# DeltaNet's inversion fed from keys and gates alone, its decays built early, and ones on TensorE in the first norm

## The chip, the cores and the metric

The kernel runs on one core of one Trainium2 chip. The metric is the device time in microseconds of one execution, the median over several. A profiled execution comes with a trace: every instruction of the engines PE (TensorE), ACT (ScalarE), DVE (VectorE) and POOL (GpSimd) and of the DMA queue SP (SyncE), with its start, duration and what ended the idle time before it.

## What is computed

A model of two layers on 512 tokens of width 1024 (batch 1): in the first a gated DeltaNet beside a dilated attention, in the second a retention beside a long convolution, and behind each a convolutional feed-forward network. The DeltaNet is what the change is about. Cut to one direction (g is the sum of the log gates within a chunk, beta the write gate):

```python
q, k, v = silu(dwconv(h @ w_in))          # q and k are normalised per head
a   = strict_lower((k * beta) @ k.T * exp(g_i - g_j))
u,w = solve(a + I, [v * beta, k * beta * exp(g)])
intra = lower(q @ k.T * exp(g_i - g_j))
for each chunk:
    v_new = u - w @ state
    o     = (q * exp(g)) @ state + intra @ v_new
    state = state * exp(g_last) + (k * exp(g_last - g)).T @ v_new
y = rmsnorm(o) * silu(z)
```

Both directions run, and their outputs are added. The result is multiplied by `ab_w_out` and added to x.

## The kernel before

**Products.** Matmuls are made exact enough by splitting each operand into a rounded part (hi) and a rest (lo); one product is three matmuls (`mm3`, L262). The activations come transposed (`hh`, `hl`). A weight tile of 128x1024 is loaded to `raw` (SP), cast to `whi` by ACT (`fetch`, L253) and `wlo` is the difference, made by DVE or, where `pool_lo` is set, by POOL (L254). There are four buffers each of `whi` and `wlo` and three of `raw`; a projection of 128 columns (`ap` or `gup`) is 24 matmuls.

**Start.** `K.start` (L190) is the one part whose instructions run in the order in which they are written. The norm's weight row is spread over 128 partitions by two matmuls with a row of ones (`nrowp`, L91), six transposes of the identity follow (`warm`, L188), each token tile is squared (ACT, L128), its factor made (POOL, L129 and L130), scaled (DVE, `xn`, L139), transposed (PE, `nt`, L152) and split (`hh` by ACT, `hl` by DVE), and the first projections (`first`) begin.

**DeltaNet.** Everywhere else a scheduler of the framework sets the order on each engine, from the order in which the code is written and the data each step needs. Twelve tiles are projected: four of keys, four of queries, four of values. Each goes through a convolution (`conv3`: ACT L362, then DVE L365 and L366), Silu (ACT), and a transpose (PE, `tp`, L685); for keys and queries the norm is squared on ACT (L692, four instructions with a sum each), its root made on POOL (L386, L387), and applied on DVE (L697). Between the value tiles stand, per chunk c, the transposes of keys and queries (L765), the products `kkp` and `kqp` (L771, L773), the decays `dps` (PE) and their Exp (ACT, L783), and `blocks` (L785): the intra-chunk matrix A (DVE, L787), P = kk·beta·decay (DVE, L791, eight small instructions per chunk) and its 32x32 blocks to `Bt` (ACT L797, DVE L799). After the last chunk comes the recursion that inverts all 32x32 blocks at once (L824 and L825, 31 steps of two instructions on DVE, each needing the one before), its two transposes Y (L829, L830), then on PE the joining of blocks to 64 and 128 (`m32`, `m32b`, `m64`, `m64b`) and the recurrence over four steps. The gate projection `pt` (96 matmuls of `proj_tok`) stands ahead of the recursion in the code. The other half of the mixer's output product (`oacc`, eight units of 12 matmuls, `fill`) is spread over the places that `FILLS` counts: three units before `m32`, two before `m32b`, and so on.

The gates themselves (`gates`, L580) end in `G4` (L646), the log gates with both signs; `gate_operands` (L651) turns that into the operands of the decays, `gst` (eight ACT instructions, L672) in a buffer of `raw`.

## Time and profile before

| | us |
|---|---|
| median of 3 runs | 1341.88 (1340.59 to 1343.12) |
| the profiled execution | 1342.41 |
| its span, first to last instruction | 1340.6 |
| PE busy | 1311.6 (98%) |
| DVE busy | 752.0 (56%) |
| ACT busy | 531.7 (40%) |
| POOL busy | 152.8 (11%) |
| mean granted TensorE clock | 0.992 |

Busy times are of the whole span. PE has little idle time, so what the profile can show of a gain is in its waits, in its clock and in work that is taken away. The start covers 0 to 24 us of the span, the DeltaNet 139 to 345.

### The profile page before, as it was taken

What the parts mean: (1) busy time and instruction counts of PE and PEld (TensorE: products, weight loads), DVE (VectorE), ACT (ScalarE), POOL (GpSimd) and SP (SyncE); (2) the same over time, 40 slices, a digit from 0 to 9 for tenths busy, and PEclk for the clock granted to TensorE, in tenths of its full rate; (3) what the DMA queues carried; (4) which work ended last, traced back from release to release, by engine and by line L of the source; (5) the groups of instructions that cost most, each with busy time, mean ns of one, the idle gap of its engine ahead of it and who ended that gap; (6) DMA issues with size and microseconds to landing.
All of it is one profiled execution on the core that took longest, in us unless ns stands there. A gap on an engine that the chain in (4) does not pass through costs nothing.

```text
span 1340.6 us, 17716 instructions
## 1 busy us (share of the span) xinstructions
PE 1311.6 (98%) x6977; PEld 1098.2 (82%) x6977; DVE 752.0 (56%) x1106; ACT 531.7 (40%) x892; POOL 152.8 (11%) x182
## 2 busy tenths in 40 slices
PE   7999999899999999999999999999999999999997
PEld 6877887789888888888889787888898888888886
DVE  6677549968654432344436737769764443244432
ACT  4466567233443331233326424432443332133332
POOL 3454120003100000000001302024000000000002
PEclk9999999989999999999999999999999999999999
DMA  7431113221233333333333413321143333243321
GB/s 219 128 92 36 51 32 110 80 96 54 85 110 95 95 96 102 102 94 95 95 94 128 133 40 90 95 80 46 48 144 103 100 95 94 74 118 101 101 79 63
DMA packets 161027, 123.69 MB, mean 92 GB/s; under 512 B 6985, under 2 KB 134477, under 8 KB 160944
## 3 DMA queue, kind: packets, MB, share of 16 engines
q1 hardware_dynamic: 160798, 122.49, 31.2%
q8 instruction: 55, 0.90, 0.3%
q14 instruction: 28, 0.23, 0.1%
q10 hardware_dynamic: 146, 0.07, 0.0%
HBM read 117.30 MB, written 2.10 MB: 89 GB/s over the span
## 4 chain that ended last, share of the span: by engine, by line
PE 84%; DVE 8%; ACT 3%; issue 2%; DMA 1%; POOL 1%; SPq 1%; POOLq 0%; ACTq 0%; DVEq 0%
PE gup L265 11%; PE gup L266 11%; PE gup L267 11%; PE oacc L266 8%; PE oacc L265 8%; PE oacc L267 7%; PE hap L267 1%; PE ap L267 1%; PE hap L266 1%; PE ap L265 1%; PE ap L266 1%; PE hap L265 1%; PE first L266 1%; PE first L267 1%; PE first L265 1%
## 5 line engine op out<-in xcount | busy, mean ns | idle before, releaser
L254 DVE TENSOR_TENSOR wlo<-raw,whi 128x1024 fp32r<-128x1024 f32 x191 | 235.5, 1234 | 318.2 <-ACT whi L253 312.3
L253 ACT CAST whi<-raw 128x1024 fp32r<-128x1024 f32 (+1 forms) x197 | 206.5, 1049 | 432.8 <-PE gup L266 186.6
L267 PE MATMUL gup<-hh,wlo 128*128 128x512 f32 x656 | 255.6, 390 | 0.0
L266 PE MATMUL gup<-hl,whi 128*128 128x512 f32 x656 | 255.6, 390 | 0.0
L265 PE MATMUL gup<-hh,whi 128*128 128x512 f32 x656 | 255.6, 390 | 0.0
L267 PEld LDWEIGHTS gup<-hh,wlo 128*128 128x128 f32 x656 | 123.2, 188 | 25.7
L266 PEld LDWEIGHTS gup<-hl,whi 128*128 128x128 f32 x656 | 123.2, 188 | 25.3
L265 PEld LDWEIGHTS gup<-hh,whi 128*128 128x128 f32 x656 | 123.2, 188 | 25.3
L265 PE MATMUL oacc<-whi,ghi 128*128 128x512 f32 x352 | 137.3, 390 | 0.0
L267 PE MATMUL oacc<-whi,glo 128*128 128x512 f32 x352 | 137.2, 390 | 0.0
L266 PE MATMUL oacc<-wlo,ghi 128*128 128x512 f32 x352 | 137.1, 390 | 0.0
L267 PEld LDWEIGHTS oacc<-whi,glo 128*128 128x128 f32 x352 | 66.1, 188 | 13.8
L266 PEld LDWEIGHTS oacc<-wlo,ghi 128*128 128x128 f32 x352 | 66.1, 188 | 13.6
L265 PEld LDWEIGHTS oacc<-whi,ghi 128*128 128x128 f32 x352 | 66.1, 188 | 13.5
L429 DVE TENSOR_TENSOR sl<-gup,sl 128x512 f32<-128x512 f32 x42 | 29.1, 692 | 82.2 <-PE gup L267 82.2
L314 DVE TENSOR_TENSOR x<-oacc,x 128x512 f32<-128x512 f32 x64 | 43.5, 687 | 53.5 <-PE oacc L267 53.3
L428 ACT ACTIVATE sl<-c 128x512 f32<-128x512 f32 x44 | 27.8, 632 | 89.3 <-DVE c L366 89.3
L265 PE MATMUL first<-hh,whi 128*128 128x256 f32 x192 | 55.1, 289 | 0.0
L266 PE MATMUL first<-hl,whi 128*128 128x256 f32 x192 | 54.6, 285 | 0.2 <-DVE hl L226 0.2
L267 PE MATMUL first<-hh,wlo 128*128 128x256 f32 x192 | 54.5, 284 | 0.0
L265 PE MATMUL pt<-whi,hh 128*128 128x512 f32 x128 | 50.4, 394 | 3.7 <-ACT rt L454 2.5
L104 POOL TENSOR_SCALAR ss<-ss 128x1 f32<-128x1 f32 x16 | 5.0, 311 | 429.3 <-ACT jk L102 429.3
(403 smaller groups left out, 2361.9 us busy)
## 6 DMA issues: line engine op xcount, KB each, us to landing
raw<-in_ffn_w_in_dram SPq DMA_DIRECT2D x88, 512.0 KB, 3.9
raw<-in_ffn_w_out_dram SPq DMA_DIRECT2D x44, 512.0 KB, 3.7
raw<-in_ab_w_in_dram SPq DMA_DIRECT2D x28, 512.0 KB, 3.8
raw<-in_cd_w_in_dram SPq DMA_DIRECT2D x24, 512.0 KB, 4.0
x<-in_x_dram SPq DMA_DIRECT2D x16, 256.0 KB, 5.9
raw<-in_ab_w_out_dram SPq DMA_DIRECT2D x8, 512.0 KB, 3.7
raw<-in_cd_w_out_dram SPq DMA_DIRECT2D x8, 512.0 KB, 3.8
rs<-rt SPq DMA_DIRECT2D x48, 64.0 KB, 2.0
```

Source lines behind the costliest of these rows:

```text
L104: nc.gpsimd.tensor_scalar(ss[:, 1:2], ss[:, 0:1], s, EPS, op0=ALU.add, op1=ALU.add)
L253: self.nc.scalar.copy(hi, raw)
L254: (self.nc.gpsimd if self.pool_lo else self.nc.vector).tensor_tensor(lo, raw, hi, op=ALU.subtract)
L265: mm(out, a[0], b[0], start=start, stop=False)
L266: mm(out, a[0], b[1], start=False, stop=False)
L267: mm(out, a[1], b[0], start=False, stop=stop)
L314: self.nc.vector.tensor_add(xs, acc, xs)
L428: nc.scalar.activation(sl, c, AF.Silu)
L429: nc.vector.tensor_mul(sl, up, sl)
```

## The change

Four edits, of which the diff below shows the core.

- In the first norm the vector of ones is a 128x128 tile, and PE multiplies it by itself 6 times ahead of `nrowp`, 5 times behind it and 7 times behind the first transposes (`WARM`), in place of the six transposes of the identity. ACT loads the norm row before the identity and runs a 4-column Square (`tab`) before x arrives. The first weight's `wlo` is made by DVE in two halves between the scalings.
- Beta goes into the exponent of the decays (`gnl` = Ln of 1 + e), so P is one multiplication per direction and chunk, and the state's key factor takes beta (`eRb`); the multiplication of `vn` by beta becomes a copy on ACT. The mask of the diagonal goes.
- The sum of squares is one ACT instruction and a reduction on DVE.
- The DeltaNet's steps are written in another order: `gate_operands` and all decays behind the second key tile, with the decays put where A will stand; keys' products and P beside the query tiles; the recursion behind the value tiles and the gate projection in the code; A made in place beside the value tiles. `FILLS` puts no unit before `m32` and one at each later place.

```diff
         for h in range(2):
             p = k.wk(nm="nrowp")
...
+        k.warm_up(one, WARM[1])
...
+        n.scale(1, (0,))
+        lo = self.fetch(2)
+        n.turn(0, (0,))
+        self.warm_up(n.one, WARM[2])
+        lo.pop(0)()
+        n.turn(1, (0,))
+        n.scale(1, (1,))
+        n.turn(0, (1,))
+        lo.pop(0)()
+        n.turn(1, (1,))
...
+        nl = T("gnl")
+        nc.scalar.activation(nl, e, AF.Ln)
...
-            for cc in range(4):
-                jk = self.sm.tile([128, 128], F32, tag="jk2", name="jk2", bufs=1)
-                nc.scalar.activation(jk, tp[:, cc, :], AF.Square, accum_out=ss[:, cc:cc + 1])
+            nc.scalar.activation(jk, tp, AF.Square)
+            V.tensor_reduce(ss, jk, axis=AX.X, op=ALU.add)
...
-                    for h in range(4):
-                        V.scalar_tensor_tensor(P[d][:, 4 * c + h, :], kks[c][:, h, :], self.beta[:, c, 4 * d + h:4 * d + h + 1], dt[:, h, :], op0=ALU.mult, op1=ALU.mult)
+                    V.tensor_tensor(P[d][:, 4 * c:4 * c + 4, :], kkp, dt(c, d), op=ALU.mult)
...
+            tile(1, 0)
+            self.gate_operands(dp)
+            tile(1, 1)
+            turn()
             for c in range(4):
...
                 decays(c)
-                blocks(c)
+            for h in (2, 3):
+                tile(1, h)
+                turn()
+            tile(0, 0)
+            turn()
+            self.pool_lo = True
+            tile(0, 1)
+            turn()
+            for c in range(4):
+                heads_t(kT, Kt, c)
+            blocks(0)
+            tile(0, 2)
+            turn()
+            blocks(1)
+            blocks(2)
+            tile(0, 3)
+            turn()
+            blocks(3)
+            self.pool_lo = False
...
+            for h in range(4):
+                tile(2, h)
+                turn()
+                if h:
+                    attend(h)
+            turn()
+            attend(0)
+            self.proj_tok(n, lambda t, a: nc.scalar.activation(Zt[:, t, :], a, AF.Silu))
             for j in range(31):
...
-                    V.tensor_tensor(vn[d], vp, bc(self.beta[:, c, 4 * d:4 * d + 4, None], [128, 4, 128]), op=ALU.mult)
+                    nc.scalar.copy(vn[d], vp)
...
-FILLS = (3, 2, 0, 1, 1, 0, 0, 0, 1)
+FILLS = (0, 1, 1, 1, 1, 1, 1, 1, 1)
...
-WARM = 6
+WARM = (6, 5, 7)
```

`heads_t` is the old transpose of keys or queries and its copy on ACT (L768 of the changed kernel); `scores` the four products of a chunk (`kx`); `attend(c)` turns the queries, makes their products and multiplies them into the decays in place (L794 of the changed kernel).

The scheduler's order changes with the code. On PE, at the start, the rows before (`warm` on the identity, `nt` the transposes of the scaled tiles, `first` the first projection):

```order
L91 MATMUL nrowp<-nrow_97,one_99 128x512 x2
L188 MATMUL warm<-ident 128x128 x6
L152 MATMUL nt<-ident,xn 128x128 x16
L265 MATMUL first_201<-hh_133,whi 128x256
L266 MATMUL first_201<-hl_135,whi 128x256
```

and now:

```order
L192 MATMUL warm<-one_99 128x128 x6
L95 MATMUL nrowp<-nrow_96,one_99 128x512 x2
L192 MATMUL warm<-one_99 128x128 x5
L157 MATMUL nt<-ident,xn 128x128 x4
L192 MATMUL warm<-one_99 128x128 x7
L157 MATMUL nt<-ident,xn 128x128 x8
L278 MATMUL first_218<-hh_139,whi 128x256
```

Eighteen multiplications of ones stand where six transposes stood, seven of them between the first four transposes and the next eight, and the first projection begins after twelve transposes instead of sixteen.

On ACT, from the gates' Exp through the first key tiles (`eg` the gates, `scr` a tile under convolution or Silu, `jk` the squares, `whi` a weight's cast), before:

```order
L638 ACTIVATE eg<-gp 128x96
L649 ACTIVATE G_1580<-gp 128x32 x4
L362 ACTIVATE scr<-ap,dncw 128x512
L707 ACT_TABLE_LOAD
L707 ACTIVATE scr<-scr 128x512
L253 CAST whi<-raw 128x1024
L362 ACTIVATE scr<-ap,dncw 128x512
```

and the same place now, from the gates' operands on (`gx` and `gst` are these operands, `A` the tiles in which the decays are put):

```order
L231 CAST gx<-gt_1616 128x128
L689 COPY scr<-gx 32x128 x2
L728 ACT_TABLE_LOAD
L728 ACTIVATE scr<-scr 128x512
L689 COPY scr<-gx 32x128 x2
L694 ACTIVATE gst<-scr,gsel 128x128 x8
L375 ACTIVATE scr<-ap,dncw 128x512
L713 ACTIVATE jk<-tp 128x512
L260 CAST whi<-raw 128x1024
L762 ACT_TABLE_LOAD
L762 ACTIVATE A_1546<-dps 128x512
L728 ACT_TABLE_LOAD
```

The cast that stood one Silu behind the first convolution now stands behind the gates' operands, the second convolution and a Square; it is the weight of the third key tile, the next that PE projects.

On DVE, at the beginning of the recursion (`tm` and `scr` are its two instructions, L365 and L366 a convolution, `L` the transposed blocks), before:

```order
L365 SCALAR_TENSOR_TENSOR scr<-ap,dncw,scr 128x511
L812 STREAM_TRANSPOSE L<-Bt 128x1024
L366 SCALAR_TENSOR_TENSOR scr<-ap,dncw,scr 128x511
L254 TENSOR_TENSOR wlo<-raw,whi 128x1024
L824 TENSOR_TENSOR tm<-L,scr 128x31
L825 TENSOR_TENSOR scr<-scr,tm 128x31
```

and now in the middle of it (L378 and L379 are the convolution of the last value tile, L841 and L842 the recursion):

```order
L842 TENSOR_TENSOR scr<-scr,tm 128x16x16
L841 TENSOR_TENSOR tm<-L,scr 128x255
L267 TENSOR_TENSOR wlo<-raw,whi 128x1024
L378 SCALAR_TENSOR_TENSOR scr<-ap,dncw,scr 128x511
L842 TENSOR_TENSOR scr<-scr,tm 128x15x17
L379 SCALAR_TENSOR_TENSOR scr<-ap,dncw,scr 128x511
L794 TENSOR_TENSOR A_1549<-kx,A_1549 128x512
L794 TENSOR_TENSOR A_1546<-kx,A_1546 128x512
```

The last value tile's convolution, which ended before the recursion began, now stands behind 33 of its 62 instructions.

## Rows read from the trace of the kernel before

**Rows 1.** The waits of PE over the whole span, by what released it: us in total, times, longest.

```profile
PE m L855 <- DVE Y L829: 3.0, 1, 3.0
PE nt L152 <- DVE xn L139: 2.8, 1, 2.8
PE kkp L771 <- ACT kT L766: 2.1, 3, 1.4
PE pt L265 <- DVE scr L366: 1.2, 1, 1.2
```

**Rows 2.** The timeline of the start, all engines: start us, duration, engine, line, operation, and in brackets the idle time before and what ended it.

```profile
4.48 1.28 ACT L128 ACT_TABLE_LOAD   x1 [4.48 <-DMA x<-in_x_dram]
...
8.28 1.41 DVE L139 SCALAR_TENSOR_TENSOR xn<-x,ss,nrow 128x512 f32<-128x512 f32 x2
...
10.07 2.35 POOL L254 TENSOR_TENSOR wlo<-raw,whi 128x1024 fp32r<-128x1024 f32 x1
10.14 3.48 DVE L139 SCALAR_TENSOR_TENSOR xn<-x,ss,nrow 128x512 f32<-128x512 f32 x2 [0.46 <-POOL ss L130]
...
13.02 2.82 PE L152 MATMUL nt<-ident,xn 128*128 128x128 f32 x12 [2.83 <-DVE xn L139]
```

**Rows 3.** The timeline of PE at the first projection.

```profile
15.49 0.56 PE L265 MATMUL first<-hh,whi 128*128 128x256 f32 x1
...
16.49 0.28 PE L266 MATMUL first<-hl,whi 128*128 128x256 f32 x1
```

**Rows 4.** The timeline of ACT from the gates' Ln to the first key tiles, the last gate rows first.

```profile
136.72 0.58 ACT L526 COPY pT<-tp 128x512 f32<-128x512 f32 x1
...
145.72 1.28 ACT L638 ACT_TABLE_LOAD   x1
147.01 0.25 ACT L638 ACTIVATE eg<-gp 128x96 f32<-128x96 f32 x1
...
147.47 0.73 ACT L362 ACTIVATE scr<-ap,dncw 128x512 f32<-128x512 f32 x1
```

**Rows 5.** Groups of ACT from 139 to 268 us: line, engine, operation, shapes, count, busy us and mean ns of one, and idle time before.

```profile
L253 ACT CAST whi<-raw 128x1024 fp32r<-128x1024 f32 x16 | 16.8, 1052 | 19.7 <-PE ap L266 11.0 <-PE pt L267 8.6
...
L707 ACT ACTIVATE scr<-scr 128x512 f32<-128x512 f32 x9 | 5.7, 632 | 3.8 <-DVE scr L366 3.5
...
L672 ACT ACTIVATE gst<-scr,gsel 128x128 fp32r<-128x128 f32 x8 | 2.4, 388 | 0.0
```

**Rows 6.** Groups of DVE in the same stretch, same columns.

```profile
L254 DVE TENSOR_TENSOR wlo<-raw,whi 128x1024 fp32r<-128x1024 f32 x16 | 19.6, 1222 | 12.3 <-ACT whi L253 12.2
...
L791 DVE SCALAR_TENSOR_TENSOR P<-scr,beta 128x128 f32<-128x128 f32 x32 | 8.7, 346 | 0.0
L365 DVE SCALAR_TENSOR_TENSOR scr<-ap,dncw,scr 128x511 f32<-128x511 f32 x10 | 7.5, 747 | 6.2 <-ACT scr L362 6.1
...
L787 DVE TENSOR_TENSOR A<-kqp,scr 128x512 f32<-128x512 f32 x8 | 5.1, 685 | 1.6 <-ACT scr L783 1.6
L799 DVE STREAM_TRANSPOSE Bt<-P 32x128 f32<-32x128 f32 x16 | 4.8, 301 | 0.2
...
L812 DVE STREAM_TRANSPOSE L<-Bt 128x1024 f32<-128x1024 f32 x1 | 2.0, 2031 | 0.0
```

**Rows 7.** Windows of 20 us: busy us (x instructions) of PE, its weight loads, DVE, ACT, POOL, then granted clock (1.00 is 2.4 GHz, 0.50 is 1.2 GHz), DMA share, GB/s; and one window of 1 us behind the wait for the recursion.

```profile
180.00:200.00 20.00, 19.30 (x94) 15.75 (x93) 7.97 (x12) 11.94 (x45) 5.59 (x12) 1.00 0.05 14
200.00:220.00 20.00, 18.08 (x117) 15.60 (x117) 17.87 (x39) 15.40 (x30) 0.00 (x0) 1.00 0.29 82
220.00:240.00 20.00, 18.60 (x97) 15.36 (x96) 18.97 (x46) 14.68 (x25) 0.00 (x0) 1.00 0.41 130
240.00:260.00 20.00, 20.00 (x90) 16.58 (x89) 18.82 (x41) 5.44 (x7) 1.04 (x1) 1.00 0.30 84
...
277.00:278.00 1.00, 1.00 (x4) 0.81 (x3) 1.00 (x2) 0.00 (x0) 0.00 (x0) 0.50 0.16 57
```

**Rows 8.** The timeline of DVE through the recursion: its first instruction, the 34th of 62, and the transpose that PE waits for, which follows the last.

```profile
236.15 0.21 DVE L824 TENSOR_TENSOR tm<-L,scr 128x31 f32<-128x31 f32 x1
...
252.69 0.43 DVE L825 TENSOR_TENSOR scr<-scr,tm 128x255 f32<-128x255 f32 x1
...
264.47 1.90 DVE L829 STREAM_TRANSPOSE Y<-scr 128x1024 f32<-128x1024 f32 x1
```

**Rows 9.** The timeline of PE at the same place: fills before the wait, the joining of blocks, fills behind it.

```profile
261.66 0.39 PE L265 MATMUL oacc<-whi,yh 128*128 128x512 f32 x1
...
263.02 0.39 PE L265 MATMUL oacc<-whi,yh 128*128 128x512 f32 x1
266.43 2.00 PE L855 MATMUL m<-Y,P 32*32 32x32 f32 x64 [3.02 <-DVE Y L829]
...
276.47 0.63 PE L265 MATMUL oacc<-whi,yh 128*128 128x512 f32 x1
...
278.60 0.63 PE L267 MATMUL oacc<-whi,yl 128*128 128x512 f32 x1
```

**Rows 10.** The timeline of PE: the transposes behind two tiles that are five tiles apart.

```profile
163.50 0.60 PE L685 MATMUL tp<-ident,scr 128*128 128x128 f32 x4
...
193.09 0.60 PE L685 MATMUL tp<-ident,scr 128*128 128x128 f32 x4
```

**Rows 11.** The group of PE from 139 to 268 us for the keys' products of the four chunks (columns as in rows 5).

```profile
L771 PE MATMUL kkp<-kT 128*128 128x128 f32 x32 | 4.5, 285 | 2.1 <-ACT kT L766 2.1
```

More of the change, by code (lines that the diff above doesn't have):

```diff
@@ L85, in spread @@
         nc.scalar.dma_start(row, self.src)
-        one = k.sm.tile([1, 128], F32, tag="jk2", name="one1", bufs=1)
+        nc.scalar.dma_start(k.ident, k.I["ident"])
+        one = k.sm.tile([128, 128], F32, tag="jk2", name="one1", bufs=1)
         nc.vector.memset(one, 1.0)
+        nc.scalar.activation(k.sm.tile([128, 4], F32, tag="ss", name="tab", bufs=8), one[:, :4], AF.Square)
+        self.one = one
+        k.warm_up(one, WARM[0])
         self.w = k.cst.tile([128, D], F32, tag="nrow", name="nrow")
@@ L90, in spread @@
             p = k.wk(nm="nrowp")
-            nc.tensor.matmul(p, one, row[:, h * 512:h * 512 + 512], start=True, stop=True)
+            nc.tensor.matmul(p, one[:1], row[:, h * 512:h * 512 + 512], start=True, stop=True)
             nc.vector.tensor_copy(self.w[:, h * 512:h * 512 + 512], p)
+        k.warm_up(one, WARM[1])
     def square(self, t, c0=0):
@@ L136, in scale @@
         xn = self.xn[t]
-        for h in range(2):
+        for h in hs:
             sl = slice(h * 512, h * 512 + 512)
@@ L182, in new_x, with warm_up @@
         return self.cst.tile([128, NT, D], F32, tag="x", name=nm)
-    def warm_up(self, n):
+    def warm_up(self, one, n):
         p = self.wk((128, 128), "warm")
         for _ in range(n):
-            self.nc.tensor.transpose(p, self.ident, self.ident)
+            self.nc.tensor.matmul(p, one, one, start=True, stop=True)
     def start(self, n):
@@ L195, in start @@
         n.spread()
-        self.warm_up(WARM)
         n.whole(0)
@@ L253, in fetch @@
             self.nc.scalar.copy(hi, raw)
+            n = shape[1] // max(parts, 1)
+            cut = [slice(n * i, n * i + n) for i in range(parts)]
+            later = [lambda c=c: self.nc.vector.tensor_tensor(lo[:, c], raw[:, c], hi[:, c], op=ALU.subtract) for c in cut]
+            if parts:
+                self.ready.append((hi, lo))
+                return later
             (self.nc.gpsimd if self.pool_lo else self.nc.vector).tensor_tensor(lo, raw, hi, op=ALU.subtract)
@@ L754, in deltanet @@
             Ai = [dp.tile([128, 2, 4, 128], F32, tag="ai", name=f"A{st}", bufs=4) for st in range(4)]
-            prep = self.delta_prep(dp, n, gates, Kt, Qt, Vt, Zt)
-            next(prep)
-            self.gate_operands(dp)
+            tile, turn = self.delta_tiles(dp, n, gates, (Qt, Kt, Vt))
             Bt = self.xp.tile([128, 32, 32], F32, tag="xn", name="Bt")
-            kks, kqs, dts = {}, {}, {}
-            def turn(c):
-                for out, src in ((kT, Kt), (Qt, Qt)):
-                    tp = self.wk((128, 4, 128), "tp")
-                    for h in range(4):
-                        nc.tensor.transpose(tp[:, h, :], src[:, c, h, :], self.ident)
-                    nc.scalar.copy(out[:, c], tp)
-            def products(c):
-                kkp, kqp = self.wk((128, 4, 128), "kkp"), self.acc((128, 4, 128), "kqp")
-                for h in range(4):
-                    nc.tensor.matmul(kkp[:, h, :], kT[:, c, h, :], kT[:, c, h, :], start=True, stop=True)
-                for h in range(4):
-                    nc.tensor.matmul(kqp[:, h, :], kT[:, c, h, :], Qt[:, c, h, :], start=True, stop=True)
-                kks[c], kqs[c] = self.s2h("kk"), kqp
-                V.tensor_tensor(kks[c], kkp, bc(self.tri[:, 4:5, :], [128, 4, 128]), op=ALU.mult)
+            dt = lambda c, d: Ai[3 - c if d else c][:, d]
             def decays(c):
@@ L781, in decays, with heads_t, scores @@
                     nc.tensor.matmul(ps, self.gst[:, 4 * d + c, :], self.gmv, start=False, stop=True)
-                    dts[c, d] = self.s2h("dt")
-                    nc.scalar.activation(dts[c, d], ps, AF.Exp)
+                    nc.scalar.activation(dt(c, d), ps, AF.Exp)
+            def heads_t(out, src, c):
+                tp = self.wk((128, 4, 128), "tp")
+                for h in range(4):
+                    nc.tensor.transpose(tp[:, h, :], src[:, c, h, :], self.ident)
+                nc.scalar.copy(out[:, c], tp)
+            def scores(c, x):
+                ps = self.acc((128, 4, 128), "kx")
+                for h in range(4):
+                    nc.tensor.matmul(ps[:, h, :], kT[:, c, h, :], x[:, c, h, :], start=True, stop=True)
+                return ps
             def blocks(c):
+                kkp = scores(c, kT)
                 for d in range(2):
-                    V.tensor_tensor(Ai[3 - c if d else c][:, d], kqs[c], dts[c, d], op=ALU.mult)
+                    V.tensor_tensor(P[d][:, 4 * c:4 * c + 4, :], kkp, dt(c, d), op=ALU.mult)
                 for d in range(2):
-                    dt = dts[c, d]
-                    for h in range(4):
-                        V.scalar_tensor_tensor(P[d][:, 4 * c + h, :], kks[c][:, h, :], self.beta[:, c, 4 * d + h:4 * d + h + 1], dt[:, h, :], op0=ALU.mult, op1=ALU.mult)
                     for q in range(4):
```

88 lines of the change are left out of this document (30 added, 58 removed).

## The prediction

> **What bounds the kernel now.** The table says PE, at 98% of the span, so I read PE's waits first and then, at each of them, the engine that PE waits for. Five waits matter, and four of them stand where the change works [rows 1]: 2.8 us for the second scaled tile at the start, then in the DeltaNet 3.0 us for the recursion's transpose, 2.1 us for the copies of turned keys on ACT and 1.2 us for the last value tile's convolution. The start is read from the timeline [rows 2, 3], the DeltaNet from its windows and groups. What the reader is to see in the windows is DVE: from 200 to 260 us it is busy 17.87, 18.97 and 18.82 of each 20 us [rows 7]. The recursion is one chain on it, from 236.15 us to the transpose at 264.47 [rows 8]. PE covers that chain with the gate projection and with fills, of which the last starts at 263.02, and then stands still until 266.43 [rows 9]. That wait has a second price. Fills that started 0.227 us apart before it (1.36 us for six) start 0.426 us apart behind it (2.13 for five): the granted clock is 0.50 there, the lower of its two levels, 1.2 GHz instead of 2.4 [rows 7]. Fifteen of the fills run there, 15 x 0.20 = 3.0 us. So before loses 6.3 us in three waits and 3.0 us to the clock behind one.
>
> **The start.** Three things get shorter. The table load of 1.28 us stands ahead of the first Square, behind x's arrival [rows 2]; the small Square draws it before x is there. The norm's row is loaded first. The second scaling took 3.48 us beside POOL's `wlo` of 2.35, where the same two instructions took 1.41 us alone [rows 2]; with `wlo` on DVE that neighbour is gone, and two halves, 1.22 us in all [rows 6], stand between the scalings. Against that stand the seven ones between the first transposes and the next. A multiplication of 128x128 in full precision is not in the start; the nearest is the keys' product, 4.5 us for 16, so 0.28 us each [rows 11], and twice that at the lower clock: 2.0 to 3.9 us for seven. They begin when the first four transposes are done: 10.2 us now (13.02 less the wait of 2.83), 9.8 with the norm's row 0.4 us sooner. At the upper clock they end near 11.8, the next transposes start 1.2 us before the 13.02 us of now [rows 2], and the first projection, which needs four transposes fewer, 0.4 us sooner still. At the lower clock they end near 13.7 and the gain is gone. The first projection's matmuls also begin at half speed, 0.56 us long against 0.28 soon after [rows 3]; without the 2.83 us wait in front this is worth some 0.4 us. I take -2.0, between -3.5 and +0.7.
>
> The Trainium skill (SBUF — State Buffer, "Who interferes with whom") says that a DVE instruction with two inputs in SBUF and a reading GpSimd instruction block each other for whole instructions; the 3.48 beside 2.35 agrees. It also speaks against a later part of this change, since three weights of the DeltaNet go to POOL: by that rule each could hold DVE up to 2 us. These fall before the queries' second tile, where DVE is busy 7.97 of 20 us [rows 7], so I give it nothing.
>
> **The end of the dilated attention.** Two more table loads, for the new Ln and back, of 1.28 us each and an instruction of some 0.23 us now stand ahead of ACT's last copy at 136.72 [rows 4]. PE's last products wait for that copy. Half of the 2.8 us should lie in ACT's waits for DVE there; I take +0.6, from 0 to +1.8. The Trainium skill (ScalarE: Activation LUTs, "What ACT_TABLE_LOAD costs") counts a drain of about 1.4 us on each switch besides the load; the row at 145.72 shows 1.28 us and the next instruction at 147.01, so this trace does not show it. With it this term and the next would each be larger by some 2.8 us.
>
> **Decays in the keys' tiles.** Here ACT is the chain. From the gates' Exp to the cast of the third key tile's weight it has to run: Exp 0.25, a convolution 0.73 [rows 4], two short copies and two signs of the gates, about 0.5, the rounding of the turned gates 0.3, four copies 1.2, a table load 1.28, a Silu 0.63, `gst` 2.4, a convolution 0.7, the Square of 128x512 (by the Silu of the same size 0.6), and the cast 1.05 [rows 5]: 9.6 us from 147.1, and about 0.8 us for the way to DVE and PE and back in the middle. The cast ends near 157.5. PE takes 29.59 us for five tiles with their turns, 5.92 each, of which 24 x 0.227 = 5.45 is the tile [rows 9, 10]; the first turn, two periods ahead of 163.50, stands at 151.7. With its 0.5, the 0.6 from above, one more transpose of 0.3 and three decays of two matmuls, 1.4, PE arrives near 154.5. It waits 3.0 us. `wlo` follows by DVE, 1.22 us, of which one matmul covers 0.2: +1.0. The cast for the fourth tile stands behind eight Exp, a Silu and three table loads, 9.2 us; it comes 1.0 us late. Together +5.0; if ACT's chain is covered in part +2.5, if DVE is busy at the `wlo` +7. In before all these casts were done tiles ahead, since ACT had waited 11.0 us for PE to free a buffer [rows 5]. That cover is gone once `gst` and the order put the cast last. A wait of three microseconds brings the clock down as the one above did; for its length I take half of that price, +1.5, from 0 to 3.0.
>
> **From the second query tile to the gate projection.** This is the term that decides. PE has six tiles with turns, 35.5; two more turns and eight transposes of heads at 0.47, 4.7; eight sets of products, at 4.5/4 with the overlap of their ends off some 0.9, 7.2: 47.4 us in all [rows 9 to 11]. DVE has in the same stretch, up to the last value tile's convolution, which the order now puts behind 33 recursion instructions: seven `wlo` 8.6; fourteen convolution halves 10.5; eight P at 0.685 (the size of A's instruction) 5.5; sixteen block transposes 4.8; L 2.0; four A 2.7 [rows 6]; four scalings at the same 0.69, 2.8; four reductions of 128x512, not in the trace, bounded by 0.35 (the small P) and 0.75 (a convolution half) and taken at 0.68, the two-operand instruction of that size, 2.7; and of the recursion the stretch from 236.15 to 253.12 less the four `wlo` in it (some 1.14 each) and one instruction that the trace shows too long, 11.6 [rows 8]. Sum 51.2 us. Then follow Silu 0.63, two transposes 0.94, a copy 0.58 and a set of products 0.9 before the projection may start: 3.05. If DVE never waited, PE would lose 51.2 + 3.05 - 47.4 = 6.9 us. In the stretch that is fullest now it is busy 92.8% [rows 7]; at that share 51.2 take 55.2 us and PE loses 10.9. At the lowest of the three windows, 89%, it is 13. I take 10.9, from 6.9 to 13. The projection's 96 matmuls, 21.8 us, then cover what is left of the recursion (28 instructions, some 11 us, and one `wlo`) and its transposes, 3.1 us, so the wait for Y goes, as the change says. The stop before the projection costs clock: +1.5, from 0 to 3.0.
>
> **Taken away.** The three waits, 6.3 us, and the 3.0 us of clock behind the recursion: -9.3. The mask of the diagonal, the smaller P (8.7 us to 5.5) and the Square's sums are in DVE's and ACT's sums above. The copy of `vn` on ACT in place of DVE's multiplication is two of each kind per step, of one length; the fills, now one per gap, cover it and the short waits behind the recursion stay: 0.
>
> Sum: -2.0 + 0.6 + 5.0 + 1.5 + 10.9 + 1.5 - 9.3 = +8.2 on the profiled execution's 1342.4, so 1350.6; that execution is 0.5 us above the median of the runs: 1350.1.
>
> **Rivals.** First, PE keeps going: DVE runs near its 51.2 us because its queue is never empty, and the reductions cost 0.35. For it speaks that the recursion, a chain before, now has other work between its steps; against it that four conversions per tile (ACT's convolution, Square, POOL's root, the scaling) stand in DVE's queue in order, each a wait. With no stop long enough to cost clock, -2.5 + 0.3 + 2.5 + 5.6 - 9.3 = -3.4: 1338.5, faster. Second, things cancel: ACT's chain and DVE's queue lie near their lower ends, -2.0 + 0.6 + 2.5 + 7.5 + 0.5 - 9.3 = -0.2: 1341.7. For it speaks that PE, late by the decays, gives DVE time before the stretch begins. Third, slower still, and from the clock: PE, stopped at each value tile, stays at the lower level into the gate projection, whose 96 matmuls then run 0.20 us longer each until it rises. With 3.0 us there, 3.0 at the decays, 13 in the stretch and no gain at the start: 0.6 + 5.0 + 3.0 + 13 + 3.0 - 9.3 = +15.3, 1357.2. It decides from the point at which the stops come every six microseconds. Fourth, the change does what it says (the inversion ends under the projection) but the ones don't raise the clock: the start gives +0.3 and the time is 1352.4; that is in the forecast's own range.
>
> **Chances.** Forecast 0.50, the fourth 0.08, the third 0.07, the first 0.21, cancelling 0.14. A measurement tells 0.2%, 2.7 us, from no change. So faster 0.21, same 0.13, slower 0.66 (some of the cancelling case lies above the bound). The forecast's own range is 1344 to 1356: the ends of its terms, not all at once. The range that should hold 8 in 10 reaches down into the first rival and up to the third: 1337.5 to 1357.
>
> **What would show it.** Start: the first projection near 13.5 us instead of 15.49, with matmuls of 0.28 us at once; seven ones of 0.5 us would show the lower clock. Decays: PE waits for ACT `whi` between the second and third key tile, about 3 us. Stretch: PE waits for ACT Silu of value tiles, 9 us or more in total, and m32 no longer waits for Y, which is ready 7 us or more before it. If the waits of PE in the DeltaNet come to less than 9 us in all, the forecast is wrong; if DVE's queue is busy under 85% from the second query tile on, I was wrong about what limits it.

## The result, and the profile after

| | before | after |
|---|---|---|
| median of 4 runs each, us | 1342.43 (1340.59 to 1343.12) | 1351.68 (1350.64 to 1354.71) |
| ratio | | 1.0075 [1.0055, 1.0094] |
| the profiled execution, us | 1342.41 | 1354.71 |
| its span, us | 1340.6 | 1352.9 |
| mean granted clock | 0.992 | 0.990 |

The changed kernel is slower by 9.3 us; 1350.1 was forecast. The profiled execution of after is the slowest of its four, 3.0 us above their median, so its trace holds some 3 us more than has to be explained.

PE's waits over the whole span (engine, line, what released it: us in total, times, longest), to hold against [rows 1]:

```profile
PE kx L773 <- ACT qtok L768: 5.0, 4, 1.6
PE tp L707 <- ACT scr L728: 4.0, 3, 2.2
PE pt L278 <- ACT rt L467: 3.2, 2, 1.6
PE ap L278 <- ACT whi L260: 2.4, 1, 2.4
...
PE tp L537 <- ACT pT L539: 1.4, 1, 1.4
...
PE op L548 <- ACT pT L539: 0.9, 1, 0.9
...
PE ap L280 <- DVE wlo L267: 0.9, 1, 0.9
```

The wait for the recursion (3.0) and the one for the scaled tile (2.8) are gone. In their place PE waits for ACT's copies of the turned queries, `qtok`, in front of each chunk's product `kx`, for the Silu of the value tiles (`scr`), and for a weight's cast.

The timeline of the start of after, all engines, to hold against [rows 2, 3]:

```profile
7.40 1.41 DVE L144 SCALAR_TENSOR_TENSOR xn<-x,ss,nrow 128x512 f32<-128x512 f32 x2 [0.55 <-POOL ss L135]
...
9.13 2.73 PE L192 MATMUL warm<-one 128*128 128x128 f32 x14
9.58 0.75 DVE L144 SCALAR_TENSOR_TENSOR xn<-x,ss,nrow 128x512 f32<-128x512 f32 x1 [0.77 <-POOL ss L135]
...
11.70 1.04 PE L157 MATMUL nt<-ident,xn 128*128 128x128 f32 x8
...
12.98 0.39 PE L278 MATMUL first<-hh,whi 128*128 128x256 f32 x1 [0.24 <-ACT hh L231]
```

Each scaling now takes 0.75 us at most, and the first projection begins 2.5 us sooner. The gain does not last. The dilated attention's `pt` begins at 40.75 instead of 41.48: by then 1.8 of the 2.5 us are gone, since the first projections wait 0.9 us for `hl` in three places (0.2 before) and four of the transposes now stand among them. `pt` then waits 1.61 us instead of 0.74 for ACT's `rt`, and the next step, `sp`, begins at 64.42 against 64.28.

PE at the key tiles, where the decays now stand:

```profile
160.99 0.50 PE L278 MATMUL ap<-hh,whi 128*128 128x512 f32 x1 [2.37 <-ACT whi L260]
162.75 0.79 PE L280 MATMUL ap<-hh,wlo 128*128 128x512 f32 x1 [0.87 <-DVE wlo L267]
```

PE from the second query tile's turn to the gate projection `pt`:

```profile
190.93 0.60 PE L707 MATMUL tp<-ident,scr 128*128 128x128 f32 x4
...
223.64 0.66 PE L707 MATMUL tp<-ident,scr 128*128 128x128 f32 x4 [2.21 <-ACT scr L728]
...
226.12 1.96 PE L773 MATMUL kx<-qtok,kT 128*128 128x128 f32 x8 [1.10 <-ACT qtok L768]
...
236.84 1.16 PE L773 MATMUL kx<-qtok,kT 128*128 128x128 f32 x8 [1.58 <-ACT qtok L768]
...
245.92 1.16 PE L773 MATMUL kx<-qtok,kT 128*128 128x128 f32 x8 [1.60 <-ACT qtok L768]
248.62 0.66 PE L707 MATMUL tp<-ident,scr 128*128 128x128 f32 x4 [1.54 <-ACT scr L728]
...
250.44 2.08 PE L773 MATMUL kx<-qtok,kT 128*128 128x128 f32 x8 [0.73 <-ACT qtok L768]
...
252.17 0.77 PE L278 MATMUL pt<-whi,hh 128*128 128x512 f32 x1
```

That is 61.2 us for the 47.4 us of work that the prediction counted: 13.8 lost, 9.7 of them in waits. The windows of after (columns as in [rows 7]):

```profile
160.00:180.00 20.00, 18.00 (x69) 13.88 (x70) 9.39 (x12) 17.38 (x24) 3.40 (x5) 0.83 0.30 82
...
220.00:240.00 20.00, 15.03 (x73) 12.17 (x72) 18.30 (x38) 7.26 (x12) 1.46 (x3) 0.91 0.24 72
240.00:260.00 20.00, 16.14 (x80) 13.46 (x79) 17.61 (x41) 5.37 (x8) 0.00 (x0) 0.91 0.11 33
```

and one window over the whole stretch:

```profile
191.00:252.00 61.00, 51.26 (x272) 42.76 (x271) 51.21 (x99) 28.23 (x53) 5.82 (x12) 0.96 0.21 65
```

DVE, the third pair, is busy 51.21 of 61.0 us, 84%. The granted clock was 1.00 in the windows of [rows 7] and is 0.91 here; over the stretch it is 0.96. If the rest is time at the lower level of 1.2 GHz, that is 8% of the 61 us, 4.9, at half speed, which costs 2.4. Waits and clock together are 12.1 of the 13.8 us; the rest lies in the count of the work, as the run with the pipelining alone shows below.

DVE at the last value tile's convolution (L378, L379) and at the end of the recursion (L841, L842; Y its transposes):

```profile
246.11 0.74 DVE L378 SCALAR_TENSOR_TENSOR scr<-ap,dncw,scr 128x511 f32<-128x511 f32 x1
246.77 0.41 DVE L842 TENSOR_TENSOR scr<-scr,tm 128x255 f32<-128x255 f32 x1
247.10 0.74 DVE L379 SCALAR_TENSOR_TENSOR scr<-ap,dncw,scr 128x511 f32<-128x511 f32 x1
...
262.94 2.13 DVE L846 STREAM_TRANSPOSE Y<-scr 128x1024 f32<-128x1024 f32 x1
264.99 1.20 DVE L847 STREAM_TRANSPOSE Y<-scr 128x1024 f32<-128x1024 f32 x1
```

Y is ready at 266.19; `m32` begins at 274.77 without a wait, 8.6 us later. Before, it began at 266.43 [rows 9]. What that is worth shows in the joining of blocks itself. The first line is before's window behind its wait, the second the first instructions of after's `m32` (`m`):

```profile
266.00:279.00 13.00, 12.57 (x236) 10.17 (x237) 9.76 (x13) 6.62 (x7) 0.00 (x0) 0.50 0.62 205
```

```profile
274.77 2.00 PE L872 MATMUL m<-Y,P 32*32 32x32 f32 x128
```

In before 64 of these small matmuls take 2.00 us [rows 9], in after 128 do, at a granted clock of 1.00 (window 274 to 294 us). So the low clock in before slowed these products as much as the fills, and PE was busy for 12.57 of these 13 us.

### The profile page after: what moved, and what is told of

Same layout as the page of the kernel before. It is cut to its first block, busy times and chain, and to the rows that moved or that the text cites. A ratio compares the mean times of both kernels' runs of the same rounds, so it can differ in the third digit from the quotient of the medians.

```text
span 1352.9 us, 17724 instructions
## 1 busy us (share of the span) xinstructions
PE 1317.7 (97%) x7007; PEld 1101.5 (81%) x7007; DVE 740.8 (55%) x1081; ACT 532.8 (39%) x848; POOL 157.9 (12%) x184
## 4 chain that ended last, share of the span: by engine, by line
PE 83%; DVE 7%; ACT 4%; issue 2%; DMA 2%; POOL 1%; SPq 1%; POOLq 0%; ACTq 0%; DVEq 0%
PE gup L279 11%; PE gup L278 11%; PE gup L280 11%; PE oacc L278 8%; PE oacc L280 7%; PE oacc L279 7%; PE pt L278 2%; PE pt L280 2%; PE pt L279 2%; PE hap L279 1%; PE hap L278 1%; PE hap L280 1%; PE ap L278 1%; PE ap L280 1%; PE ro L1065 1%
## 5 line engine op out<-in xcount | busy, mean ns | idle before, releaser
L267 DVE TENSOR_TENSOR wlo<-raw,whi 128x1024 fp32r<-128x1024 f32 x188 | 231.6, 1234 | 324.4 <-ACT whi L260 317.2
L280 PEld LDWEIGHTS oacc<-whi,glo 128*128 128x128 f32 x352 | 66.1, 188 | 13.8
```

The costliest lines, as they stand in the source:

```text
L267: (self.nc.gpsimd if self.pool_lo else self.nc.vector).tensor_tensor(lo, raw, hi, op=ALU.subtract)
L280: mm(out, a[1], b[0], start=False, stop=stop)
```

## The experiments

In the expectations, theory A is the ledger of the prediction as the trace of after corrects it: no lasting gain at the start, the late casts as the price of the decays, and DVE's queue as what sets the stretch before the gate projection. The rivals are described there, and theory D in the text where it first stands. The expectations call the runs by number: e1 is the start alone, e2 all but the start, e7 the pipelined version with casts ahead and fills, e10 that version with L's transpose later. Ratios are against runs of before on the same chip.

### The start alone, and all but the start

Before with the start's edits (`one`, `tab`, the order of loads and turns, `WARM`):

```diff
...
-WARM = 6
+WARM = (6, 5, 7)
```

> The kernel before with the start of the changed kernel alone (ones, norm row first, early table load, the first low weight in halves). Theory A: the first projection begins about 2.5 us earlier, but the next wait of PE, for ACT's rotated tile ahead of the gate-less projection of the dilated part, grows and gives it back: 1341 to 1343, no change that can be told. Rival B: the upstream delay of the changed kernel (its first key tile begins 4.2 us later than before) comes from this start: 1345 to 1347. Rival C: the gain lasts: 1339.5 to 1340.5.

1344.15 (1340.47 to 1346.52), ratio 1.0013 [1.0003, 1.0024]: no gain, if anything 1.7 us lost; the time lies above theory A's range and below rival B's. B is out by the trace: the first key tile begins at 138.21, not later than before's 138.98. The run's profiled execution is the fastest of the twelve and shows `first` at 12.57 and `sp` at 63.59, so 0.7 us are left of 2.9 where the dilated attention's products begin.

After with before's start:

```diff
...
-WARM = (6, 5, 7)
+WARM = 6
```

> The changed kernel with the start of the kernel before. Theory A: 1350 to 1353, as changed. Rival B: 1347 to 1348.5, since the delay ahead of the DeltaNet goes. Rival C: 1353.5 to 1354.5.

1351.28 (1350.13 to 1354.78), ratio 1.0073 [1.0057, 1.0089], 0.4 us from after. The start is worth nothing in either kernel. The 1.4 us wait of `tp` for `pT` near 85 us stands here too, so it isn't the start's either.

Later the first of these was run without the ones:

```diff
-WARM = (6, 5, 7)
+WARM = (0, 0, 0)
```

> The kernel of e1 (the start alone) without any multiplication of ones. If the ones keep the clock up: the first transposes and the first projection run at the lower level, matmuls of 0.56 us where e1 has 0.28, for 1 us or more, and the granted clock of the first projection's beginning is under 1.00 or its spacing 0.21 us; the first projection begins no earlier than 13.0 us. If they only fill PE's waits and hold up the second transposes: it begins 0.5 to 1 us sooner than e1's, and the time is within 2 us of e1's.

1343.78 (1340.88 to 1345.94), ratio 1.0009 [0.9997, 1.0021]: the ones change nothing that shows. PE's timeline of this run says why:

```profile
11.70 0.58 PE L280 MATMUL first<-hh,whi 128*128 128x256 f32 x1
...
13.44 0.41 PE L282 MATMUL first<-hh,wlo 128*128 128x256 f32 x1
13.66 0.41 PE L280 MATMUL first<-hh,whi 128*128 128x256 f32 x1
...
16.65 0.28 PE L282 MATMUL first<-hh,wlo 128*128 128x256 f32 x1
```

Without ones the projection begins 0.9 us sooner than in the first run, at 11.70 against 12.57, and runs its matmuls 0.21 us apart until 16.65; with ones they stand 0.12 us apart from 13.5 on, with gaps in which PE waits for `hl`. The ones buy the clock with the time in which they run. Of the first expectation the spacing of 0.21 us came, the late beginning (13.0 or later) did not.

### The new Ln behind the old one

Meant to take two of the added table loads away: the Ln for beta is written right behind the Ln of the gates.

```diff
-        nl = T("gnl")
-        nc.scalar.activation(nl, e, AF.Ln)
+        nl, e2 = T("gnl"), T("ge2")
...
         nc.scalar.activation(g, u, AF.Ln)
+        nc.scalar.activation(nl, e, AF.Ln)
```

> The changed kernel with the new Ln behind the Ln that was there, so that two table loads of 1.28 us go. Theory A: the wait of PE's last products of the dilated part for ACT's copy, 0.9 us, goes and nothing else: 1350.5 to 1351.2. Rival: the switches cost more than their rows show (a drain each), and 2.5 us or more go: under 1349.5.

1352.13 (1348.32 to 1355.14), ratio 1.0076 [1.0060, 1.0092], as after, with the same wait of 0.9 us of `op` for `pT`. But ACT's timeline shows that the edit did not do what it was written for:

```profile
139.71 1.28 ACT L633 ACT_TABLE_LOAD   x1
141.00 0.23 ACT L633 ACTIVATE gnl<-ge 128x32 f32<-128x32 f32 x1
141.25 1.28 ACT L629 ACT_TABLE_LOAD   x1
...
142.68 0.57 ACT L539 COPY pT<-tp 128x512 f32<-128x512 f32 x1
```

The scheduler puts the Ln (L633) where its operand is ready, ahead of the Exp (L629), as in after; both loads still stand in front of the last copy of `pT`. The run says nothing on their price. That the copy waits for these two loads is read from the rows, not tested.

### Two casts ahead of the decays

```diff
             tile(1, 0)
+            self.fetch()
+            self.fetch()
             self.gate_operands(dp)
```

> The changed kernel with two more weights fetched ahead of the gates' operands, so that ACT casts them before the eight operand instructions, the second convolution and the Exp. Theory A: PE's waits for the third key tile's cast and low part (2.4 and 0.9 us) and the clock behind them go, and since DVE is under half busy there the gain stays: 1346.5 to 1348.5. Rival: the later stretch paced by DVE takes it back: 1350.5 to 1352.

1347.84 (1342.64 to 1348.89), ratio 1.0038 [1.0026, 1.0050], 3.8 us below after. PE no longer waits for `whi`, only 0.2 us for a `wlo`, and the clock stays up where it was 0.83:

```profile
160.00:180.00 20.00, 19.57 (x91) 15.86 (x92) 8.99 (x13) 16.66 (x24) 8.59 (x7) 1.00 0.39 106
```

From the first key tile to the second query tile's turn, the stretch with the decays, this run takes 42.0 us (140.26 to 182.26), after 47.8 (143.16 to 190.93): 5.8 less. That is the price of the late casts, waits and clock, at 5.8 instead of 6.5. The stretch behind it gives 1.2 back: 62.4 us to the gate projection instead of 61.2, with `kx` waiting 4.9 us as in after and a mean granted clock of 0.91 instead of 0.96.

Its first key tile also comes 2.9 us sooner than in the profiled execution of after. There a weight's cast stands at 81.61 us, behind the two casts of `dq` on ACT, and PE's `tp` waits 1.4 us for `pT`; in this run the cast stands at 78.69, ahead of them, as at 78.83 in before, and `tp` waits 0.8. The order of the casts, moved in one place, moved there too.

### The recursion behind the last value tile

A one-column copy of the last value tile's convolution into `tm` holds the recursion back. By theory A the projection should start at the pace of a DVE without those 33 instructions.

```diff
             self.conv3(c, ap, cw, (f, 12 + f, 24 + f))
+            if f == 11:
+                nc.vector.tensor_copy(self.tm[:, :1], c[:, :1])
...
```

> The changed kernel, with the recursion held until the last value tile's convolution is done on DVE (a one-column copy of that tile into the recursion's scratch ties them). Theory A (PE loses before the gate projection because the value tiles stand behind the recursion in DVE's queue): PE's waits for the value tiles' Silu, 4.0 us, go, the projection begins about 53 us behind the second query tile instead of 61; the recursion ends later and PE waits 4 to 6 us for Y, which was hidden before: 1347 to 1350.5. Rival (PE loses there to the copies of turned queries on ACT, 5.0 us of waits, whatever DVE does): the projection begins 60 us or more behind that tile, and with the new wait the time is 1354 to 1358.

1363.38 (1359.10 to 1364.33), ratio 1.0149 [1.0131, 1.0168], above the ranges of both. DVE at the last value tile, ACT there, and PE's waits from 180 to 300 us:

```profile
242.79 1.23 DVE L267 TENSOR_TENSOR wlo<-raw,whi 128x1024 fp32r<-128x1024 f32 x1 [5.02 <-ACT whi L260]
...
244.72 0.75 DVE L379 SCALAR_TENSOR_TENSOR scr<-ap,dncw,scr 128x511 f32<-128x511 f32 x1
```

```profile
241.71 1.05 ACT L260 CAST whi<-raw 128x1024 fp32r<-128x1024 f32 x1 [4.59 <-PE ap L279]
```

```profile
PE kx L775 <- ACT qtok L770: 4.9, 4, 1.6
PE tp L707 <- ACT scr L730: 4.0, 3, 2.2
PE m L874 <- DVE Y L848: 2.4, 1, 2.4
```

DVE now has 41.3 us of work in the stretch instead of 51.2 and stands idle for 5.02 us in front of the last tile. Yet the convolution ends 57.1 us behind the second query tile's turn (188.38), in after 56.9, and `pt` begins at 251.46, 63.1 us behind it, in after 61.2. PE's two waits are the same to a tenth. So the step "the queue's order puts the last convolution behind 33 recursion instructions, and that sets the projection's start" is false: DVE waited for ACT's cast, and that for a buffer which PE's `ap` frees. (The copy that holds the recursion also holds the last Silu, by 0.9 us; without it the projection would begin 62 us behind the turn.) The recursion moved back is then paid behind the projection, by more than the rival counted: `m` waits 2.4 us for Y and begins 27.9 us behind `pt`, in after 22.6.

### All value tiles' `wlo` on POOL

The other way to take work from DVE: `pool_lo` stays on through the value tiles and the gate projection.

```diff
             blocks(3)
-            self.pool_lo = False
...
             self.proj_tok(n, lambda t, a: nc.scalar.activation(Zt[:, t, :], a, AF.Silu))
+            self.pool_lo = False
```

> The changed kernel with the low parts of the value tiles' and the projection's weights on POOL too, so that DVE has six or seven times 1.22 us less in the stretch that it is said to pace. Theory A with POOL and DVE side by side: the projection begins 6 to 8 us earlier: 1344 to 1347. Rival (the two block each other, as the 3.5 us of the scaling beside POOL's 2.35 at the start): recursion instructions beside POOL's take 1 to 2 us instead of 0.4 and the gain is lost: 1351 to 1356.

1360.35 (1357.88 to 1360.95), ratio 1.0129 [1.0114, 1.0145], above the rival's range too. The wait of `tp` for Silu grows from 4.0 to 10.6 us, 7.15 of it once, and `pt` begins 66.9 us behind the turn. POOL and DVE (two views) show a cause:

```profile
243.73 2.35 POOL L267 TENSOR_TENSOR wlo<-raw,whi 128x1024 fp32r<-128x1024 f32 x1 [8.54 <-ACT whi L260]
```

```profile
243.89 2.47 DVE L842 TENSOR_TENSOR scr<-scr,tm 128x255 f32<-128x255 f32 x1
...
251.10 0.74 DVE L378 SCALAR_TENSOR_TENSOR scr<-ap,dncw,scr 128x511 f32<-128x511 f32 x1
```

A recursion instruction that took 0.41 us in after (246.77) takes 2.47 beside POOL's 2.35, and the recursion then runs on, ahead of the convolution that PE waits for. Here DVE's order does decide. By the Trainium skill (SBUF — State Buffer, "Who interferes with whom") a DVE instruction with two inputs in SBUF contends with a GpSimd instruction that reads SBUF, and the second to issue waits; these rows agree, with POOL at 243.73 and DVE at 243.89.

### Queries turned one tile ahead of their products

If PE's own order is the cause, writing each chunk's transposes of queries a tile ahead of the products removes the waits for `qtok`, and the last turn behind the gate projection removes the last wait for Silu. Run first with the casts ahead, the Ln as written above and two fills in front of `m32`:

```diff
             def attend(c):
-                heads_t(Qt, Qt, c)
...
+            heads_t(Qt, Qt, 2)
+            attend(1)
+            tile(2, 3)
+            turn()
+            heads_t(Qt, Qt, 3)
+            heads_t(Qt, Qt, 0)
+            attend(2)
+            attend(3)
             attend(0)
             self.proj_tok(n, lambda t, a: nc.scalar.activation(Zt[:, t, :], a, AF.Silu))
+            turn()
...
-FILLS = (0, 1, 1, 1, 1, 1, 1, 1, 1)
+FILLS = (2, 1, 1, 1, 1, 0, 0, 1, 1)
```

> The changed kernel with the weights fetched ahead, the Ln behind the other Ln, the queries' transposes written one tile ahead of their products, the last value tile's transpose behind the gate projection, and two fills ahead of the joining of blocks. Theory A: the waits for copies of queries go, but the last convolution still stands behind 27 recursion instructions, so the projection begins about 54 us behind the second query tile: 7 us less than as changed, and 4 us from the weights: 1340 to 1343. Rival (these waits are hidden behind DVE's queue anyway): 1347 to 1349.

1340.72 (1335.62 to 1343.55), ratio 0.9986 [0.9974, 0.9997]: 11.0 us below after, and just below before. PE's waits from 180 to 300 us:

```profile
PE tp L707 <- ACT scr L728: 2.4, 2, 2.2
PE pt L278 <- DVE scr L379: 0.5, 1, 0.5
...
PE kx L773 <- ACT qtok L768: 0.3, 1, 0.3
```

The projection begins 53.5 us behind the turn (181.64 to 235.11), with the recursion still ahead of the last convolution on DVE. `m32` begins at 263.02 without a wait, Y having ended at 259.02. The last wait in front of `pt` is now for DVE's last convolution, 0.5 us.

The same with the recursion held back as above:

```diff
...
+            if f == 11:
+                nc.vector.tensor_copy(self.tm[:, :1], c[:, :1])
...
```

> The same with the recursion held until the last value tile's convolution is done. Theory A: DVE has 42 us of work up to there instead of 51, PE does not wait before the projection, which begins 48 to 50 us behind the second query tile, and the projection with two fills covers the recursion to within 2 us: 1334 to 1338, faster than both kernels. Rival: the recursion, now all behind, ends 6 us or more after the fills, and the clock falls as in the kernel before: 1341 to 1345.

1348.47 (1344.91 to 1350.68), ratio 1.0043 [1.0028, 1.0059], above both ranges. The stretch shortens by another 2.4 us, to 51.1, where in after the same edit shortened nothing: with the queries turned ahead, DVE's queue is the limit that is left. But `m` waits 2.5 us for Y, `m32b` 1.5, and the clock falls to 0.80 from 260 to 280 us. The early recursion is worth more than the convolution in front of which it stands.

After with the pipelining alone, that is without the casts ahead and the moved Ln, its `FILLS` as in after (none in front of `m32`):

> The changed kernel with one edit: the queries' transposes written one tile ahead of their products, and the last value tile's transpose behind the gate projection. Theory D (PE stops before the gate projection for ACT's copies of the queries that it turned just before, and for the clock that such stops cost, while DVE's queue has room): the waits for these copies, 5.0 us in all, go, the projection begins 53 to 55 us behind the second query tile instead of 61: 1343.5 to 1346. Theory A (DVE's queue sets the pace): its order up to the last convolution is nearly the same, and the projection begins within 2 us of where it did: 1349.5 to 1351.5.

1353.09 (1350.45 to 1353.99), ratio 1.0073 [1.0057, 1.0088]. The stretch is 53.5 us here too (192.70 to 246.16), 7.7 less than in after, with the waits for `qtok` down from 5.0 to 0.3 us, the length that theory D gave. Two things make it up. The last convolution ends 53.4 us behind the turn instead of 56.9, and what in after lies between its end and `pt` (Silu, turn, copy, product), 4.3 us, now stands behind the projection. DVE runs 27 recursion instructions ahead of that convolution's second half instead of 34, and `pt` waits 1.8 us for it, so its queue sets the beginning here. Yet the time is above the ranges of both theories, and between the medians nothing is gained. PE at `m32`:

```profile
269.00 0.28 PE L881 MATMUL m<-Y,P 32*32 32x32 f32 x4 [0.30 <-DVE Y L855]
270.12 1.18 PE L881 MATMUL m<-Y,P 32*32 32x32 f32 x50 [0.84 <-DVE Y L856]
273.84 2.01 PE L881 MATMUL m<-Y,P 32*32 32x32 f32 x74 [2.54 <-ACT vtok L709]
```

The projection ends before Y does. PE waits for both halves of Y and for ACT's copy of the last value tile, which this edit put behind the projection, and the clock is 0.83 from 260 to 280. Counted from the first key tile (145.31 here, 143.16 in after), `vnp` comes at 151.8 us, in after at 153.9: 2.1 of the 7.7 us are left there, the others came back as these waits and their clock.

This run also shows what PE's work in the stretch takes by itself. The granted clock is 1.00 over all of it, and PE waits 2.4 us for Silu, 1.8 for DVE's last convolution, 0.7 for `kT` and 0.3 for `qtok`: 53.5 less 5.2 is 48.3, and 48.8 with the one turn (0.47) that stands behind the projection here. The prediction had counted 47.4.

Against this run the first pipelined version is 10.3 us shorter from the first key tile to the transposes of the next norm (196.8 against 207.1). Of that, 5.4 lie ahead of the second query tile's turn, where its casts are moved, and 4.9 behind the projection's beginning, where its fills are. The fills alone were not run.

### L's transpose behind the first value tile's convolution

L's transpose, 2.10 us, runs ahead of the first value tile's convolution, whose Silu PE waits 2.2 us for. Here, in the pipelined version, a one-column copy ties it behind.

```diff
             self.conv3(c, ap, cw, (f, 12 + f, 24 + f))
+            if f == 8:
+                nc.vector.tensor_copy(self.L0, c[:, :1])
...
```

> The pipelined kernel of e7, with the transpose L (2.1 us of DVE) tied behind the first value tile's convolution. Theory D: the one long wait of PE that is left there, 2.2 us for that tile's Silu, shrinks to under 0.5, and about 1 us of clock behind it comes back: 1337 to 1339.5. Theory A: the work is the same, only in another order, and the last convolution moves by nothing: 1340 to 1341.5.

1341.01 (1339.14 to 1346.21), ratio 0.9996 [0.9985, 1.0008]: no change against the pipelined version's 0.9986. The wait grew to 3.6 us, by the experiment's own doing:

```profile
217.00 0.63 ACT L730 ACTIVATE scr<-scr 128x512 f32<-128x512 f32 x1 [4.03 <-DVE L L729]
```

Silu overwrites what the small copy (L729) reads, and the copy stood at 216.76, behind a scaling that waits for POOL. The run tells nothing of L. The same with before's start:

```diff
...
-WARM = (6, 5, 7)
+WARM = 6
```

> The same with the start of the kernel before. If the start of the changed kernel gains nothing that lasts (as in e1 and e2): within 2 us of e10. If it gains its 2.5 us once PE is not stopped later: 2 to 3 us above e10.

1340.94 (1338.61 to 1344.80), ratio 0.9989 [0.9978, 1.0000]: the medians differ by 0.1 us, so the start is worth nothing here either.

## Why the prediction was right, and where it was not

**The sum** came out: 1350.1 against 1351.68, slower as forecast. By landmarks of the profiled execution the terms were these.

| term | forecast | measured |
|---|---|---|
| start | -2.0 | +0.1 where `sp` begins; +0.1 to +1.7 between medians |
| dilated attention's end | +0.6 | at the first key tile, less the start: +4.0 in after, +2.4 with before's start, +1.4 with the casts ahead |
| decays, with clock | +6.5 | +5.8 (casts ahead) |
| stretch to the projection, with clock | +12.4 | +13.8 over the 47.4 us of work counted; 12.4 over the 48.8 measured |
| waits and clock taken away | -9.3 | -5.6 in waits (0.7 of the keys' copies, `kT`, stay) and about -6.3 in clock |

The measured terms, with +4.0 and +13.8, add up to 11.8. The profiled execution is 11.1 us late at the next norm's first transposes (341.19 before, 352.29 after) and 12.3 at its end, part of it at a wait of 1.4 us in the feed-forward network (`hm`) that before does not show; the medians are 9.3 apart. That the sum came so near is luck in part: the start and the dilated attention's end cost more than forecast, and more was taken away.

**The start.** The view of what happens there was right: 12.98 was measured for "near 13.5", the neighbour POOL gone, the seven ones at 2.73 us between the bounds of 2.0 and 3.9. The failed step is that a sooner projection moves the end. Behind it lie more waits for `hl` (0.9 us for 0.2) and a wait for ACT's `rt`, which grew from 0.74 to 1.61 us and took the rest of the gain. A term at the start counts only as far as the next wait behind it.

**The dilated attention's end.** The picture was right: `op` waits 0.91 us for the copy behind two table loads, where +0.6 was forecast; taking the loads away was tried and didn't come about. What is more than that comes in part from a place that the prediction did not look at: `tp` near 85 us, 0.6 us later for a cast that moved behind `dq`, and in this one execution the clock at 0.83 from 80 to 90 us, where the run with before's start shows the same wait and 1.00. The two runs differ by 1.6 us there. Some 0.5 to 0.7 us are left without a cause.

**The decays.** Right in place and size: 2.37 us for `whi` (3.0 forecast), 0.87 for `wlo` (1.0), the clock down (0.83 from 160 to 180 us); with two casts written ahead 5.8 us came back in this stretch and 3.8 between the medians. The wait of 1.0 us at the fourth tile did not come.

**The stretch.** The size was right, 12.4 over the work as measured, and so were DVE's pieces: 0.676 us for a reduction taken at 0.68, P at 0.681 for 0.685, and the convolution's end 56.9 us behind the turn where 55.2 was worked out. The reason does not hold as given, so that the size is luck in part. The prediction gave DVE's queue as the limit, and PE's waits as Silu of value tiles, 9 us or more. Measured were 4.0 for Silu and 5.0 for the copies of queries turned just before, a wait that the prediction did not price, although its kind stands in [rows 1] as 2.1 us for `kT`. Its own sign against itself, DVE below 85%, came out at 84%, and holding the recursion back settled it: 10 us less work on DVE, and the same convolution end, 57.1 us behind the turn. So a chain around PE alone takes that long: tile, turn, copy on ACT, product, each waiting for the one before, with the clock low in between. With the recursion held in both, turning the queries a tile ahead brings that end from 57.1 to 50.9 us (the casts ahead, which that run has besides, do not shorten it by themselves: 57.3). With the recursion in place it comes at 53.4, and DVE's queue is the limit. In after the two limits lie close together; taking away either the recursion alone or the chain alone gives nothing or 3.5 us of the 6. The other 4.3 us lie behind the convolution, where the prediction had 3.05.

**The inversion under the projection.** Right: no wait at `m32`, Y 8.6 us ahead (7 or more forecast). The run with the pipelining alone shows how: the time that PE lost in front of the projection is part of the time in which the recursion was hidden. With it gone, Y comes too late unless fills stand in front of `m32`, as two do in the version that ends below before.

**Waits and clock taken away.** The three waits were priced rightly; the clock behind the recursion was not. The prediction charged the low clock to fifteen fills, 3.0 us. The window from 266 to 279 us shows 12.57 us of PE's work at 0.50, and the 128 small matmuls of `m32` took 3.9 us there against 1.9 in after. At half speed the whole of it costs about 6.3 us (estimated from that window), 3.3 more than counted.

**The rivals.** The first, in which PE keeps going, is what the pipelined version with fills comes near to, 1340.7 where 1338.5 was worked out, but not for the reason given: not a DVE without idle time, which is busy 45.4 of 53.5 us there, but an order of PE without products behind fresh copies. The third did not come: from 254 us on the granted clock is 1.00, so the projection runs fast. The fourth, ones that don't lift the clock, is wrong in its mechanism: the seven ones run for the most part at the low clock (0.50 from 8 to 11 us), but behind them matmuls of 256 columns take 0.28 us from 13.92 on. Its result for the start, no gain, is what came.

## What to carry to other kernels

When a sum over one engine's work gives the length of a stretch, look at what the other engine waits for before calling that engine the limit: taking work off it and seeing nothing move is the test. It has to be made again when the other limit is gone: there the same edit moved 2.4 us. On an engine that works in order, a transpose, its copy elsewhere and the product of it need something between them, or each is a wait, of 0.7 to 1.6 us here, and here it cost clock too (0.91 from 220 to 260 us). Work hidden behind a stall is not free when the stall is removed; put the cover back (here two fills) in the same step. And when a wait brings the clock down, charge the low clock to all that PE does until it rises, not to one kind of its work.

## What the runs showed of the hardware

At the start the granted clock of the windows did not always tell the speed. In the run without ones it reads 1.00 from 12 to 16 us, while matmuls of 256 columns stand 0.21 us apart, against 0.12 from 16.65 on:

```profile
12.00:16.00 4.00, 3.85 (x17) 3.49 (x16) 2.65 (x5) 1.54 (x3) 0.00 (x0) 1.00 1.05 384
```

There the spacing of equal matmuls is to be read. In the run of the start with ones the windows agree with it: 0.53 from 8 to 11 us and 1.00 from 11 on. Ones multiplied by ones did bring the speed up for what followed: in after eight matmuls of the second transposes take 1.04 us from 11.70 on, where before's twelve took 2.82 [rows 2]. And in after waits of 0.7 to 2.2 us, none longer, stood in two windows of 20 us whose granted clock is 0.91; in the pipelined version a window with one wait of 2.2 us and one of 0.2 (200 to 220 us) reads 0.91 as well.
